# Running-ahead distances per stage, 24 whole fp32 columns in layer 1, and 32 gathers moved ahead, in a two-layer diffusion block with a product-key expert layer

## The chip, the cores and the metric

The kernel runs on one NeuronCore of one Trainium2 chip. The metric is the device time of one execution in microseconds; lower is better. The profile is one execution with a hardware trace. Engines are called as the profile calls them: PE is TensorE, DVE is VectorE, ACT is ScalarE, POOL is GpSimd, SP is SyncE.

## What is computed

Two layers of a block act on 256 latent tokens `x` and 256 context tokens `ctx`, each 1024 wide, all in fp32. Each layer has modulation from a condition vector, a mixer with three branches (differential attention, window attention with grouped heads, gated DeltaNet in chunks of 64), a gated merge, and an expert layer. The second layer updates the latent only; of the context it needs keys, values and the DeltaNet state.

```
for l in range(DEPTH):
    need_ctx = l < DEPTH - 1
    ...
    m, mc = token_mixer(h, hc, ...)
    x = x + gt1 * m
    x = x + gt2 * peer_ffn(modulate(x, norm2_g[l], sh2, sc2), peer_wq[l], peer_keys[l],
                           peer_u[l], peer_v[l])
    if need_ctx:
        xc = xc + gt1c * mc
        xc = xc + gt2c * peer_ffn(...)
return x
```

The expert layer `peer_ffn` picks, for each token and each of 8 heads, 16 of 16384 experts (top 16 of 128 first keys and of 128 second keys, then top 16 of the pairs), and returns the sum over experts e of softmax weight times gelu(h . u[e]) times v[e].

## The kernel before

The program is written as plain code against a recorder, `Rec`, which stands for the five engines. It notes each operation with its operands; `order()` is a list scheduler that then sets the order in which the operations of each engine are issued, and `emit()` issues them all from one line, L627. So every row of the trace has that line, and tiles tell the operations apart. `ps` is PSUM, `b` is a working tile in SBUF, `rows` a tile of 128 gathered table rows.

The scheduler goes by estimated costs and a priority: the place in the program, plus `base` (RBASE = -8000 makes routing urgent). An operation ahead of the oldest unfinished one of its lane is put off if it needs a tile and is further ahead than a distance (`FAR`, 80 units of estimated work), or if, beyond `NEAR` (20), it would leave fewer tiles than SPARE of its tag. Tags are b4 (36 tiles of 4 KB a partition), b2, b1 and ps (8 PSUM banks); `rows` and `ga` borrow slots of b4.

The stages in `run`: modulation of layer 0; the context through layer 0 (norm, projections by `w_in`, branches, merge, output projection); `peer_front`, the context's routing; `mix(0,0)`, the latent through layer 0; the latent's expert layer `peer_dense(0,0)`; layer 1 (`add_peer`, norm, keys, values and state of the context, then `mix(1,0)` and `peer_dense(1,0)` of the latent).

The context's experts (`peer_gather`) are lane -1, run beside the latent's work. For a block of 128 tokens, U gathers 128 times 128 rows of the first table (512 KB each, indirect DMAs that POOL issues); DVE multiplies each with h and sums. V then forms the weights `cf`, transposes them, gathers 128 times from the second table, PE multiplies with a selector `Z` (`ps<-rows,ga`), and ACT copies the result to a tile that SP stores in DRAM (`xd<-ga`). The order is U(0), V(0), U(1), V(1). `add_peer` of layer 1 loads what V stored.

The latent's experts are computed densely: for each of 128 columns (first keys), dU computes gelu of all 256 tokens against 128 rows of u, G (the weight of each token and expert, made in the stage "build" from one-hot rows by small matmuls and written to DRAM as `gd`) multiplies it on DVE, and dV multiplies with 128 rows of v. `pre` columns of dU (32 in layer 0, PRE1 = 64 in layer 1) stand ahead of the first dV.

A load in fp32 is mostly split: ACT casts it to the high half in fp32r, DVE subtracts to get the low half, and PE does three fp32r matmuls (`mm3`) for each product. A column in `u4` is left whole instead: one fp32 matmul against the unsplit transposed norm `hT[k][2]`, which the trace shows as two records. Before, `U4 = range(32)` makes the first 32 columns of layer 0 whole and layer 1 has none. In `first` of `peer_dense`:

```
if c0 in u4:
    for k in range(KT):
        nc.tensor.matmul(sp[:, i], u[:, k], hT[k][2], start=(k == 0), stop=(k == KT - 1))
    continue
uh, ul = self.split(u, ...)
self.mm3(sp[:, i], lambda k: (uh[:, k], ul[:, k]), lambda k: hT[k])
```

Of the kernel before, what the change touches and what calls it, by code (L numbers as in the profile page):

```python
# [41 lines left out]
WN = 32  # L42
U4, V4 = range(32), ()
WPOOL = ()
UP0, UP1 = (), ()
PRE1 = 64
# [7 lines left out]
GBASE, RBASE = 0, -8000  # L54
TAIL, FREE1 = 0, True
FREE = {"b4": 4, "b2": 2, "b1": 1, "ps": 0}
PRE = 32
LOAD = {"tensor": 1.0, "vector": 0.3, "scalar": 0.2}
NEAR, FAR, URGENT = 20.0, 80.0, 0.0

# [210 lines left out]
class Op:  # L271
    __slots__ = ("i", "eng", "meth", "args", "kw", "dur", "dma", "preds", "succ", "tiles", "prio",
                 "npred", "ready", "lab", "lane", "cw", "port", "free")

# [12 lines left out]
class Rec:  # L287
# [5 lines left out]
    def __init__(self, nc, pools, bufs):  # L293
        self.nc, self.pools, self.bufs = nc, pools, bufs
        self.ops, self.tiles = [], []
        self.tensor, self.vector = Eng(self, "tensor"), Eng(self, "vector")
        self.scalar, self.gpsimd, self.sync = Eng(self, "scalar"), Eng(self, "gpsimd"), Eng(self, "sync")
        self.base = 0
        self.lane, self.cw, self.free = 0, {}, False
        self.lab = ""  # L300
        self.why, self.prevt, self.inslot, self.fin = {}, {}, {}, {}
# [47 lines left out]
    def add(self, eng, meth, args, kw):  # L349
        o = Op()  # L350
# [36 lines left out]
        o.preds = list(preds)  # L387
        o.lane, o.free = self.lane, self.free
        o.cw = self.cw[o.lane] = self.cw.get(o.lane, 0.0) + o.dur * LOAD.get(eng, 0.0) * (URGENT if self.base == RBASE else 1.0)
# [14 lines left out]
    def order(self):  # L404
# [89 lines left out]
        def blocked(o):  # L494
            for t in o.tiles:
# [7 lines left out]
                if f > front:  # L503
                    keep = 0
                    if o.lane >= 0:
                        head = ops[lanes[o.lane][lpos[o.lane]]]
                        dist = o.cw - head.cw
                        free = o.free and lpos[-1] >= len(lanes[-1]) - TAIL
                        if dist > FAR and not free:
                            return "far"  # L510
                        if free and dist > NEAR:
                            keep = FREE.get(t.tag, 0)
                        elif dist > NEAR or o.lane != main:
                            keep = SPARE.get(t.tag, 0) + (LOADS if o.dma and t.tag == "b4" else 0)
                    if load[t.tag][front:f].max() + 1 > cap[t.tag] - keep:
                        return t.tag
# [114 lines left out]
class Kern:  # L631
# [1058 lines left out]
    def peer_gather(self, l, s, F):  # L1690

        nc = self.nc
        out = self.dram_x()
        for b in range(NB):
            self.lab(f"{l}{s} U{b}")
            dots = self.t("pdot", [P, P], bufs=1)
            h2 = self.t("ga", [P, D], bufs=3)
            nc.sync.dma_start(h2, F["hd"][b * P:(b + 1) * P, :])
            for j in range(P):
                r, _ = self.gather(self.I["u_tab"], F["eid"][j // 32][:, b].rearrange("p h k -> p (h k)")[:, j % 32:j % 32 + 1])  # L1700
                nc.vector.scalar_tensor_tensor(r, r, 1.0, h2, op0=OP.mult, op1=OP.mult, accum_out=dots[:, j:j + 1])
            self.lab(f"{l}{s} V{b}")
            cf = self.t("pcf", [P, P], bufs=2)
            nc.scalar.activation(cf, dots, AF.Gelu)
            nc.vector.tensor_tensor(cf, cf, F["gw"][:, b].rearrange("p h k -> p (h k)"), op=OP.mult)
            pt = self.ps([P, P], tag="psg")
            nc.tensor.transpose(pt, cf, self.id)
            cT = self.t("pcfT", [P, 4, 32], bufs=1)
            nc.scalar.copy(cT, pt.rearrange("p (q j) -> p q j", q=4))


            po = [self.ps([P, 512], tag="psg") for _ in range(2)]
            for j0 in range(0, 32, 8):
                Z = self.t("ga", [P, 8, 4, 32], bufs=3)
# [11 lines left out]
            acc = self.t("ga", [P, D], bufs=3)  # L1726
            for hf in range(2):
                nc.scalar.copy(acc[:, hf * 512:(hf + 1) * 512], po[hf])
            nc.sync.dma_start(out[b * P:(b + 1) * P, :], acc)
        return out  # L1730

# [39 lines left out]

    def run(self):
        self.setup()
        self.silu_c()
# [15 lines left out]
        if ADA1 == 4:  # L1790
            self.fill = fill
        self.whole = True
        _, (x, xs) = self.mix(0, 0, self.I["x"], pr, kv, S)
        self.whole = False
        self.dump("x0", x)
        self.layer_rows(1, pr1)
        self.nc.lane, self.nc.base = -1, GBASE
        acc = self.peer_gather(0, 1, F)
# [9 lines left out]
        self.lab("1 norm1")  # L1808
        self.nc.free = FREE1
# [4 lines left out]
        self.nc.free = False  # L1814
        _, (x, xs) = self.mix(1, 0, x, pr1, kv, S)
        self.dump("x2", x)
        self.peer_dense(1, 0, x, xs, pr1, self.out, pre=PRE1, up=UP1)

# [24 lines left out]
```

## Time and profile before

| what | value |
|---|---|
| time of the kernel, median of 3 runs | 3811.16 us (3800.89 to 3819.09) |
| the profiled execution, its own time | 3817.58 us |
| its span in the trace | 3815.8 us |
| mean granted clock of PE | 0.938 of full speed |
| PE busy | 3463.5 us (91%), 23800 instructions |
| weight loads of PE (PEld) busy | 2960.3 us (78%) |
| DVE busy | 2374.0 us (62%) |
| ACT busy | 1707.0 us (45%) |
| POOL busy | 818.8 us (21%) |
| DMA | 837.67 MB, mean 220 GB/s |

Busy shares are means over stages with different limits. So the span is cut into windows, with the busy time of each engine, the granted clock (a share of the full 2.4 GHz; 0.50 is 1.2 GHz) and the DMA share in each. The timeline lists an engine's instructions in order of time, merged when alike; brackets hold the idle time ahead of them and what ended it. "<-DVE b" means that the engine waited for DVE to write a tile `b`.

### The profile page before, as it was taken

Reading aid. Unit: us, or ns where it says so; the run is one execution under the profiler, and the core shown is the slowest. Engines: PE = TensorE matmul, PEld = TensorE weight load, DVE = VectorE, ACT = ScalarE, POOL = GpSimd, SP = SyncE. Lnnn points to the kernel's source line nnn. Section 1 sums busy time; section 2 is a strip of 40 time slices with the busy share of each in tenths; the row PEclk is TensorE's granted clock in tenths of the full one; section 3 lists DMA queues with packets and bytes.
Section 4 is the critical chain, followed back from the end, with each engine's and each line's share of the span. In section 5 each row is a group of like instructions: output and inputs, shape, how many; then the busy total and the mean of one; then the engine's idle time right before and its main releaser. Section 6 shows DMA issues by size and latency. Waiting matters only on the chain.

```text
span 3815.8 us, 62556 instructions
## 1 busy us (share of the span) xinstructions
PE 3463.5 (91%) x23800; PEld 2960.3 (78%) x23800; DVE 2374.0 (62%) x5288; ACT 1707.0 (45%) x3554; POOL 818.8 (21%) x716
## 2 busy tenths in 40 slices
PE   8999994987998987999999999998995789999999
PEld 6875993876797674788777778887795679889998
DVE  4542569887556783988544455645568963665554
ACT  4743441541543181343333347763543564444443
POOL 1010001476123434655444311101010000000000
PEclk9996997988899998999999998989997899999999
DMA  6346753597277889999899961212262364776562
GB/s 256 117 138 223 239 191 127 181 332 274 75 254 276 292 291 394 409 372 365 337 359 338 342 250 40 84 45 94 62 233 72 119 185 150 243 280 227 199 211 105
DMA packets 300956, 837.67 MB, mean 220 GB/s; under 512 B 26736, under 2 KB 96752, under 8 KB 300656
## 3 DMA queue, kind: packets, MB, share of 16 engines
q1 hardware_dynamic: 153168, 522.80, 38.6%
q0 software_dynamic: 73728, 268.47, 18.9%
q10 hardware_dynamic: 73760, 42.40, 3.7%
q8 instruction: 188, 3.08, 0.3%
q14 instruction: 112, 0.92, 0.1%
HBM read 792.67 MB, written 40.89 MB: 218 GB/s over the span
## 4 chain that ended last, share of the span: by engine, by line
PE 49%; DVE 4%; ACT 3%; issue 1%; DMA 1%; ACTq 0%; POOL 0%; POOLq 0%; DVEq 0%
PE ps L627 49%; ACT b L627 3%; DVE b L627 3%; DVE psi L627 0%; DVE psv L627 0%; ACTq L627 0%; DMA gd<-b 0%; DMA b<-in_v_tab 0%; DMA b<-in_u_cols 0%; DVE pii L627 0%; DVE pS L627 0%; DVE pci L627 0%; DVE dst L627 0%; DVE ga L627 0%; POOL qrs L627 0%
## 5 line engine op out<-in xcount | busy, mean ns | idle before, releaser
L627 PE MATMUL ps<-b,b 128*128 128x256 f32 (+4 forms) x18016 | 2761.0, 314 | 194.5 <-DVE b L627 121.6
L627 PEld LDWEIGHTS ps<-b,b 128*128 128x128 f32 (+1 forms) x18016 | 2452.5, 192 | 489.8 <-DVE b L627 141.9
L627 DVE TENSOR_TENSOR b<-b,b 128x1024 fp32r<-128x1024 f32 (+3 forms) x1218 | 1137.0, 977 | 718.5 <-ACT b L627 509.1
L627 ACT CAST b<-b 128x1024 fp32r<-128x1024 f32 (+1 forms) x918 | 850.2, 972 | 481.3 <-PE ps L627 341.0
L627 ACT COPY b<-ps 128x256 f32<-128x256 f32 (+3 forms) x896 | 289.2, 350 | 492.6 <-PE ps L627 483.5
L627 POOL DMA_INDIRECT rows<-in_u_tab,eid x256 | 349.4, 1365 | 321.5 <-DVE rows L627 232.7
L627 ACT ACTIVATE b<-ps 128x512 f32<-128x512 f32 (+1 forms) x266 | 137.5, 520 | 619.5 <-PE ps L627 609.6
L627 POOL DMA_INDIRECT rows<-in_v_tab,eidT x256 | 290.6, 1135 | 502.4 <-PE ps L627 442.4
L627 DVE SCALAR_TENSOR_TENSOR rows<-rows,ga 128x1024 f32<-128x1024 f32 x256 | 306.1, 1224 | 58.2 <-DMA rows<-in_u_tab,eid 58.2
L627 PE MATMUL ps<-consts,b 128*128 128x128 f32 (+1 forms) x1290 | 251.5, 312 | 84.1 <-DVE b L627 64.9
L627 PE MATMUL ps<-b 128*128 128x128 f32 (+1 forms) x2048 | 272.9, 301 | 37.8 <-ACT b L627 36.7
L627 PEld LDWEIGHTS ps<-b 128*128 128x128 f32 (+1 forms) x2048 | 231.6, 203 | 81.8 <-ACT b L627 60.0
L627 PEld LDWEIGHTS ps<-consts,b 128*128 128x128 f32 x1290 | 181.6, 179 | 131.9 <-issue 50.2
L627 DVE COPY_PREDICATED b<-masks,ps 128x64 f32<-128x64 uint8 (+1 forms) x416 | 83.2, 252 | 132.4 <-PE ps L627 129.4
L627 PE MATMUL ps<-rows,ga 128*32 128x512 f32 x1024 | 139.2, 599 | 7.2 <-DMA rows<-in_v_tab,eidT 7.2
L627 ACT COPY b<-b 128x128 f32<-128x128 f32 x384 | 108.0, 305 | 44.7 <-DVE b L627 42.3
L627 POOL TENSOR_TENSOR b<-b,b 128x512 f32<-128x512 f32 x24 | 45.5, 1896 | 351.7 <-DVE b L627 326.2
L627 DVE TENSOR_SCALAR b<-consts,b 128x128 f32<-128x128 f32 x384 | 110.3, 346 | 0.0
L627 DVE TENSOR_TENSOR b<-ps,b 128x128 f32<-128x128 f32 (+4 forms) x144 | 61.9, 455 | 72.3 <-PE ps L627 48.6
L627 DVE TENSOR_TENSOR b<-consts,b 128x512 f32<-128x512 f32 x128 | 87.0, 685 | 13.5 <-DMA gd<-b 8.6
L627 PE MATMUL ps<-b,cs 128*32 128x256 f32 x768 | 76.5, 460 | 11.6 <-DVE cs L627 11.6
L627 PEld LDWEIGHTS ps<-rows,ga 128*32 128x32 f32 x1024 | 29.2, 109 | 73.3 <-issue 45.0
(176 smaller groups left out, 1567.5 us busy)
## 6 DMA issues: line engine op xcount, KB each, us to landing
b<-in_u_cols SPq DMA_DIRECT2D x256, 512.0 KB, 5.5
b<-in_v_tab SPq DMA_DIRECT2D x256, 512.0 KB, 6.5
b<-in_w_in SPq DMA_DIRECT2D x184, 512.0 KB, 6.5
gd<-b ACTq DMA_DIRECT2D x64, 512.0 KB, 5.2
b<-gd SPq DMA_DIRECT2D x64, 512.0 KB, 5.7
b<-in_w_ada SPq DMA_DIRECT2D x48, 512.0 KB, 8.2
b<-in_w_ada SPq DMA_DIRECT2D x96, 256.0 KB, 4.6
b<-in_wq SPq DMA_DIRECT2D x48, 512.0 KB, 6.1
```

Of the source, the lines that this page charges most:

```text
L627: r = getattr(getattr(nc, o.eng), o.meth)(*[_real(x) for x in o.args], **{k: _real(x) for k, x in o.kw.items()})
```

## The change

First, the one distance FAR = 80 becomes a distance per stage, kept with each operation (`far`): 250 for modulation, context layer 0 and its routing; 150 for `mix(0,0)`; 200 for `peer_gather` and `peer_dense(0,0)`; 80 for layer 1's context; 150 for `mix(1,0)`; 200 for `peer_dense(1,0)`. A rule that let layer 1's context run ahead without limit once all gathers were done (`free`) is removed. Second, the first 24 columns of dU in layer 1 are whole. Third, `peer_gather` runs U(0), 32 gathers of U(1), V(0), the other 96 of U(1), V(1), with two tiles of sums in place of one, and V's weights get the urgent priority.

```diff
-U4, V4 = range(32), ()
+U4, U41, V4 = range(32), range(24), ()
...
-TAIL, FREE1 = 0, True
-FREE = {"b4": 4, "b2": 2, "b1": 1, "ps": 0}
+AHEAD = 32
...
-NEAR, FAR, URGENT = 20.0, 80.0, 0.0
+NEAR, URGENT = 20.0, 0.0
+
+FARS = (250, 150, 200, 80, 150, 200)
...
-                        free = o.free and lpos[-1] >= len(lanes[-1]) - TAIL
-                        if dist > FAR and not free:
+                        if dist > o.far:
                             return "far"
-                        if free and dist > NEAR:
-                            keep = FREE.get(t.tag, 0)
-                        elif dist > NEAR or o.lane != main:
+                        if dist > NEAR or o.lane != main:
                             keep = SPARE.get(t.tag, 0) + (LOADS if o.dma and t.tag == "b4" else 0)
...
-            dots = self.t("pdot", [P, P], bufs=1)
+                dots[b] = self.t("pdot", [P, P], bufs=2)
...
+        def V(b):
             self.lab(f"{l}{s} V{b}")
+            nc.base = RBASE
             cf = self.t("pcf", [P, P], bufs=2)
-            nc.scalar.activation(cf, dots, AF.Gelu)
+            nc.scalar.activation(cf, dots[b], AF.Gelu)
...
+        U(0, 0, P)
+        U(1, 0, AHEAD)
+        V(0)
+        U(1, AHEAD, P)
+        V(1)
...
-        self.peer_dense(1, 0, x, xs, pr1, self.out, pre=PRE1, up=UP1)
+        self.nc.far = FARS[5]
+        self.peer_dense(1, 0, x, xs, pr1, self.out, u4=U41, pre=PRE1, up=UP1)
```

The order on PE in layer 1's routing, before. `ps_5624` takes the next part of the query projection from the column of `wq` whose high half is `b4_5619` and whose low half is `b4_5620`; `ps_5817` to `ps_5840` are the first columns of dU.

```order
L627 MATMUL ps_5624_28565<-b4_5437_27974,b4_5619_28102 128x256
L627 MATMUL ps_5608_28569<-b1_5448_27145,b2_5607_28556 128x128 x4
L627 MATMUL ps_5817_28579<-b4_5436_27953,b4_5819_28168 128x256
L627 MATMUL ps_5817_28579<-b4_5437_27974,b4_5819_28168 128x256
L627 MATMUL ps_5825_28583<-b4_5436_27953,b4_5827_28212 128x256
L627 MATMUL ps_5825_28583<-b4_5437_27974,b4_5827_28212 128x256
L627 MATMUL ps_5832_28590<-b4_5436_27953,b4_5834_28259 128x256
L627 MATMUL ps_5832_28590<-b4_5437_27974,b4_5834_28259 128x256
L627 MATMUL ps_5840_28594<-b4_5436_27953,b4_5842_28305 128x256
L627 MATMUL ps_5840_28594<-b4_5437_27974,b4_5842_28305 128x256
L627 MATMUL ps_5624_28565<-b4_5436_27953,b4_5620_28845 128x256
```

The same place now; the query part is `ps_5622`, its low half `b4_5618`. The rows are the last ones ahead of the first matmul with that low half, and some of the first.

```order
L625 MATMUL ps_5622_28564<-b4_5439_27962,b4_5617_28145 128x256
L625 MATMUL ps_5606_28568<-b1_5446_26129,b2_5605_28555 128x128 x4
L625 MATMUL ps_5815_27951<-b4_5431_27964,b4_5816_27824 128x256 x4
L625 MATMUL ps_5815_27951<-b4_5430_27937,b4_5817_27911 128x256 x4
L625 MATMUL ps_5815_27951<-b4_5431_27964,b4_5817_27911 128x256 x4
L625 MATMUL ps_5819_28627<-b4_5430_27937,b4_5820_27966 128x256 x4
```

```order
L625 MATMUL ps_5836_28906<-b4_5431_27964,b4_5838_28464 128x256 x4
L625 MATMUL ps_5840_28954<-b4_5430_27937,b4_5841_28469 128x256 x4
L625 MATMUL ps_5840_28954<-b4_5431_27964,b4_5841_28469 128x256 x4
L625 MATMUL ps_5840_28954<-b4_5430_27937,b4_5842_28527 128x256 x4
L625 MATMUL ps_5840_28954<-b4_5431_27964,b4_5842_28527 128x256 x4
L625 MATMUL ps_5622_28564<-b4_5438_27953,b4_5618_28986 128x256
```

Whole columns (a row x4 is four fp32 matmuls of 256 tokens) have come ahead of the matmul with the low half: 15.5 of them by this point, all 24 by the first matmul of the build. Before, the 412 matmuls of the route and 176 of dU (7.3 columns of 24) stood ahead of the build.

The order on SP at the end of layer 0's build, before. `xd<-ga` is the store of V of block 0, `gd` is G on its way back, `in_v_tab` are rows of v.

```order
L627 DMA b4_3192_14195<-in_u_cols 128x1024
L627 DMA xd_2229_14300<-ga_2497_14289 128x1024
L627 DMA b4_3193_14302<-in_u_cols 128x1024
L627 DMA b4_3195_14304<-in_u_cols 128x1024
...
L627 DMA b4_3206_14347<-in_u_cols 128x1024
L627 DMA b4_3207_14358<-in_u_cols 128x1024
L627 DMA b4_3208_14378<-gd_2988_13185 128x1024
L627 DMA b4_3209_14380<-gd_2990_13713 128x1024
L627 DMA b4_3212_14383<-in_v_tab 128x1024
```

And now:

```order
L625 DMA b4_3206_14369<-in_u_cols 128x1024
L625 DMA b4_3207_14378<-in_u_cols 128x1024
L625 DMA b4_3208_14406<-gd_2988_13286 128x1024
L625 DMA b4_3212_14408<-in_v_tab 128x1024
...
L625 DMA b4_3258_14641<-in_v_tab 128x1024
L625 DMA b4_3261_14649<-in_v_tab 128x1024
L625 DMA xd_2229_14654<-ga_2531_14635 128x1024
L625 DMA b4_3266_14668<-in_v_tab 128x1024
```

The store now stands behind the last load of u, four loads of G and twelve of v, in place of ahead of nine loads of u.

The order on PE between the context's routing and the latent's norm in layer 0, before. `ps_1423` to `ps_1426` are the transposes of the latent's normed halves `b4_1411` and `b4_1412`; `ps_1382` is a part of the context's key scores; `ps_1405` transposes expert numbers for the gathers.

```order
L627 MATMUL ps_1423_6812<-consts_1_71,b4_1411_6089 128x128 x4
L627 MATMUL ps_1424_6819<-consts_1_71,b4_1411_6089 128x128 x4
L627 MATMUL ps_1382_6829<-b1_1201_5103,b2_1381_6815 128x128 x4
L627 MATMUL ps_1425_6837<-consts_1_71,b4_1412_6118 128x128 x4
L627 MATMUL ps_1426_6847<-consts_1_71,b4_1412_6118 128x128 x4
```

And now:

```order
L625 MATMUL ps_1423_6791<-consts_1_71,b4_1411_5675 128x128 x2
L625 MATMUL ps_1424_6796<-consts_1_71,b4_1411_5675 128x128 x2
L625 MATMUL ps_1425_6818<-consts_1_71,b4_1412_5688 128x128 x2
L625 MATMUL ps_1426_6825<-consts_1_71,b4_1412_5688 128x128 x2
...
L625 MATMUL ps_1405_6963<-consts_1_71,b1_1404_6959 128x128 x2
L625 MATMUL ps_1425_6818<-consts_1_71,b4_1412_5688 128x128 x2
L625 MATMUL ps_1426_6825<-consts_1_71,b4_1412_5688 128x128 x2
```

The transposes are now in two pieces each, and the last pieces of `b4_1412` stand behind the move of the expert numbers, which follows the last round of the search. On DVE all four scalings of the latent's norm stood ahead of the last search round; now three do.

## Rows read from the trace of the kernel before

**Rows 1.** The page's busy times, with their share of the span.

```profile
PE 3463.5 (91%) x23800; PEld 2960.3 (78%) x23800; DVE 2374.0 (62%) x5288; ACT 1707.0 (45%) x3554; POOL 818.8 (21%) x716
```

**Rows 2.** Windows, by stage; the first line names the columns.

```profile
core 0: us, PE busy (x) PEld busy (x) DVE busy (x) ACT busy (x) POOL busy (x), PEclk, DMA share, GB/s
...
650.00:1160.00 510.00, 459.91 (x3036) 394.69 (x3038) 376.92 (x819) 218.70 (x564) 219.72 (x191) 0.90 0.64 224
...
1432.00:1512.00 80.00, 56.92 (x226) 34.83 (x221) 18.71 (x31) 6.11 (x11) 37.18 (x37) 0.85 1.01 392
1512.00:1840.00 328.00, 305.02 (x1689) 260.76 (x1687) 292.49 (x430) 132.02 (x158) 172.34 (x113) 0.98 0.99 385
...
2862.00:3003.00 141.00, 81.94 (x651) 80.10 (x649) 119.07 (x528) 44.22 (x72) 0.90 (x2) 0.79 0.23 79
3003.00:3104.00 101.00, 76.47 (x534) 69.12 (x534) 88.32 (x255) 80.64 (x249) 0.00 (x0) 0.94 0.56 158
3104.00:3806.00 702.00, 700.09 (x4414) 632.60 (x4415) 374.14 (x440) 312.07 (x369) 0.00 (x0) 1.00 0.59 203
```

**Rows 3.** Waits of PE: us in total, times, the longest.

```profile
PE ps L627 <- DVE b L627: 187.0, 53, 45.5
```

**Rows 4.** Windows of five short stretches, columns as in rows 2.

```profile
310.00:350.00 40.00, 38.44 (x127) 23.61 (x128) 10.91 (x35) 13.19 (x42) 1.23 (x2) 0.50 0.20 61
350.00:385.00 35.00, 34.17 (x347) 21.95 (x348) 6.89 (x31) 11.97 (x34) 0.00 (x0) 0.85 0.95 336
900.00:1000.00 100.00, 73.56 (x345) 58.80 (x346) 77.09 (x149) 36.80 (x74) 46.41 (x42) 0.71 0.50 169
1000.00:1130.00 130.00, 130.00 (x1025) 116.56 (x1025) 72.97 (x110) 61.44 (x105) 20.22 (x15) 1.00 0.48 170
3110.00:3250.00 140.00, 140.00 (x1175) 140.00 (x1175) 62.35 (x53) 60.39 (x73) 0.00 (x0) 0.99 0.50 159
```

**Rows 5.** Timeline of PE in layer 0's expert layer: start, us, engine, what.

```profile
1199.14 14.08 PE L627 MATMUL ps<-b,b 128*128 128x256 f32 x64
```

**Rows 6.** Layer 1's routing: timeline of PE, then one DVE group by form.

```profile
2869.59 3.46 PE L627 MATMUL ps<-consts,b 128*128 128x128 f32 x16 [7.09 <-DVE b L627]
...
2966.93 28.66 PE L627 MATMUL ps<-b,b 128*128 128x256 f32 x222 [45.55 <-DVE b L627]
...
L627 DVE TENSOR_TENSOR b<-b,b 128x1024 fp32r<-128x1024 f32 x18 | 21.0, 1217 | 6.4 <-PE ps L627 6.4
```

**Rows 7.** Timeline of SP's DMA queue at the end of layer 0's build.

```profile
1432.76 0.33 SPq L627 DMA_DIRECT2D b<-in_u_cols  x1
1467.84 0.33 SPq L627 DMA_DIRECT2D xd<-ga  x1
1468.27 36.70 SPq L627 DMA_DIRECT2D b<-in_u_cols  x9
```

**Rows 8.** Timeline of PE, then DVE, in the same stretch.

```profile
1477.34 20.56 PE L627 MATMUL ps<-b,b 128*128 128x256 f32 x80 [14.75 <-DMA b<-in_u_cols]
1502.16 20.36 PE L627 MATMUL ps<-b,b 128*128 128x256 f32 x80 [4.26 <-DMA b<-in_u_cols]
...
1511.79 5.14 DVE L627 TENSOR_TENSOR b<-b,b 128x256 f32<-128x256 f32 x11 [19.45 <-DMA b<-gd]
```

**Rows 9.** DVE groups by form, 1512 to 1840 us: busy, mean ns.

```profile
L627 DVE SCALAR_TENSOR_TENSOR rows<-rows,ga 128x1024 f32<-128x1024 f32 x113 | 134.9, 1219 | 0.0
```

**Rows 10.** Timeline of POOL among the gathers of block 0's V.

```profile
1060.41 1.70 POOL L627 DMA_INDIRECT rows<-in_v_tab,eidT  x1 [68.90 <-PE ps L627]
```

**Rows 11.** Timeline of PE ahead of layer 1's context norm.

```profile
2221.87 28.30 PE L627 MATMUL ps<-b,b 128*128 128x256 f32 x192
...
2266.98 3.64 PE L627 MATMUL ps<-consts,b 128*128 128x128 f32 x16 [6.98 <-issue]
```

**Rows 12.** Timeline of PE at the end of the context's routing.

```profile
608.84 6.19 PE L627 MATMUL ps<-b,b 128*128 128x256 f32 x34 [34.08 <-DVE b L627]
...
642.10 8.01 PE L627 MATMUL ps<-b,b 128*128 128x256 f32 x46 [17.91 <-DVE b L627]
```

More of the change, by code (lines that the diff above doesn't have):

```diff
@@ L272 @@
     __slots__ = ("i", "eng", "meth", "args", "kw", "dur", "dma", "preds", "succ", "tiles", "prio",
-                 "npred", "ready", "lab", "lane", "cw", "port", "free")
+                 "npred", "ready", "lab", "lane", "cw", "port", "far")
 NAMES = []
@@ L298, in __init__ @@
         self.base = 0
-        self.lane, self.cw, self.free = 0, {}, False
+        self.lane, self.cw, self.far = 0, {}, 0.0
         self.lab = ""
@@ L387, in add @@
         o.preds = list(preds)
-        o.lane, o.free = self.lane, self.free
+        o.lane, o.far = self.lane, self.far
         o.cw = self.cw[o.lane] = self.cw.get(o.lane, 0.0) + o.dur * LOAD.get(eng, 0.0) * (URGENT if self.base == RBASE else 1.0)
@@ L1693, in peer_gather, with U @@
         out = self.dram_x()
-        for b in range(NB):
+        dots, h2 = {}, {}
+        def U(b, j0, j1):
             self.lab(f"{l}{s} U{b}")
-            dots = self.t("pdot", [P, P], bufs=1)
-            h2 = self.t("ga", [P, D], bufs=3)
-            nc.sync.dma_start(h2, F["hd"][b * P:(b + 1) * P, :])
-            for j in range(P):
+            if j0 == 0:
+                dots[b] = self.t("pdot", [P, P], bufs=2)
+                h2[b] = self.t("ga", [P, D], bufs=BORROW["ga"][1])
+                nc.sync.dma_start(h2[b], F["hd"][b * P:(b + 1) * P, :])
+            for j in range(j0, j1):
                 r, _ = self.gather(self.I["u_tab"], F["eid"][j // 32][:, b].rearrange("p h k -> p (h k)")[:, j % 32:j % 32 + 1])
-                nc.vector.scalar_tensor_tensor(r, r, 1.0, h2, op0=OP.mult, op1=OP.mult, accum_out=dots[:, j:j + 1])
+                nc.vector.scalar_tensor_tensor(r, r, 1.0, h2[b], op0=OP.mult, op1=OP.mult, accum_out=dots[b][:, j:j + 1])
+        def V(b):
             self.lab(f"{l}{s} V{b}")
+            nc.base = RBASE
             cf = self.t("pcf", [P, P], bufs=2)
-            nc.scalar.activation(cf, dots, AF.Gelu)
+            nc.scalar.activation(cf, dots[b], AF.Gelu)
             nc.vector.tensor_tensor(cf, cf, F["gw"][:, b].rearrange("p h k -> p (h k)"), op=OP.mult)
@@ L1709, in peer_gather @@
             nc.scalar.copy(cT, pt.rearrange("p (q j) -> p q j", q=4))
+            nc.base = GBASE
             po = [self.ps([P, 512], tag="psg") for _ in range(2)]
             for j0 in range(0, 32, 8):
-                Z = self.t("ga", [P, 8, 4, 32], bufs=3)
+                Z = self.t("ga", [P, 8, 4, 32], bufs=BORROW["ga"][1])
                 for j in range(8):
@@ L1725, in peer_gather @@
                             nc.tie(o, ds)
-            acc = self.t("ga", [P, D], bufs=3)
+            acc = self.t("ga", [P, D], bufs=BORROW["ga"][1])
             for hf in range(2):
@@ L1772, in run @@
     def run(self):
+        self.nc.far = FARS[0]
         self.setup()
@@ L1791, in run @@
             self.fill = fill
+        self.nc.far = FARS[1]
         self.whole = True
@@ L1796, in run @@
         self.layer_rows(1, pr1)
+        self.nc.far = FARS[2]
         self.nc.lane, self.nc.base = -1, GBASE
@@ L1808, in run @@
         self.lab("1 norm1")
-        self.nc.free = FREE1
+        self.nc.far = FARS[3]
         xs = self.add_peer(1, xc, acc, pr)
@@ L1813, in run @@
         S, _ = self.main(1, 1, hT, pr1, kv, None, False)
-        self.nc.free = False
+        self.nc.far = FARS[4]
         _, (x, xs) = self.mix(1, 0, x, pr1, kv, S)
         self.dump("x2", x)
-        self.peer_dense(1, 0, x, xs, pr1, self.out, pre=PRE1, up=UP1)
+        self.nc.far = FARS[5]
+        self.peer_dense(1, 0, x, xs, pr1, self.out, u4=U41, pre=PRE1, up=UP1)
 def body(tc, I, out, dbg=None):
```

## The prediction

> **What bounds the kernel now.** Read the busy times first: TensorE (PE) 3463.5 us of a span of 3815.8 [rows 1]. So at most 352 us of waiting can be won back; anything more must come from work removed or from the granted clock. Then take the windows, one per stage of the program [rows 2]. The reader should form span minus PE busy in each: 50 us in 650:1160, 23 in 1432:1512, 23 in 1512:1840, 59 in 2862:3003, 24 in 3003:3104 and 2 in 3104:3806. The last long stage is PE work alone, at a granted clock of 1.00; only fewer matmuls help there. The stage before it, 2862:3003, is the emptiest, and the waits say on whom: 187 us on VectorE (DVE), 45.5 of it in one piece [rows 3].
>
> **The profiled execution** took 3817.58 us, 6.4 above the median of 3811.16. The sum below is made against the former, and the 6.4 comes off at the end. A change under 0.5% (19 us) can't be told from none here.
>
> **1. 24 whole columns in layer 1.** A split column costs PE 24 fp32r matmuls; 1175 of them fill 140 us in the last stage [rows 4], 0.119 each, 2.86 a column. A whole one takes 14.08/4 = 3.52 in layer 0, where the same 64 records are four columns [rows 5]. So on PE each costs 0.66 more, 24 cost 15.8, and DVE and ACT are spared a subtraction and a cast each.
> Where it pays is layer 1's routing. Before, PE has dnorm, 412 route matmuls and the equal of 7.3 split columns ahead of the build of G. It stops 45.55 us at 2966.93 because the next matmul's low half waits behind the top-16 search on DVE [rows 6]; DVE is busy 119 of 141 us there, 21.0 of it in 18 subtractions of 128x1024 [rows 6]. In the new order 15.5 whole columns stand ahead of that matmul and all 24 ahead of the build; they need only their load and the latent's transposed tile.
> PE work from 2860 to the build then is 49 (412 x 0.119) + 84.5 (24 x 3.52) + about 5 (transposes and index moves), 138.5, plus 15 for waits that stay (7.09 before the transposes, small ones at the end [rows 6]): the build starts at about 3014 in place of 3003, some 11 to 14 us later. The columns behind the build fall from 128 - 7.3 = 120.7 to 104: 16.7 x 2.86 = 48 saved. Net **-33**. Bounds: -45 if the small waits are covered too, -20 if the loads of the 24 columns (each 512 KB; 12.6 MB in the 141 us that now move 79 GB/s) come late or the build, ACT-heavy with 80.64 of 101 us, gives something back. The two more tiles of 4 KB a partition cost nothing by themselves: their cover is the pool of 36, and if it is short, loads come later, which the -20 holds.
>
> **2. The store and the gathers around the end of layer 0's build.** SP's queue before has V of block 0's store ahead of nine loads of u columns. The store is issued at 1467.84, 35 us after the load ahead of it, and only then do the nine go out [rows 7]. PE waits 14.75 and 4.26 us for them [rows 8], and DVE's first multiply by G is at 1511.79, after a wait on G's load that stands behind the nine [rows 8]. In the new order all 32 u loads, four of G and twelve of v rows stand ahead of that store. So up to 27 us of start (1512 back to about 1485) are to be had.
> The second part is DVE in 1512:1840, busy 292 of 328, of which 113 products for the gathers take 134.9, 1.22 each [rows 9]. In the new order 96 stand there: 17 x 1.22 = 21 us less. But PE's work is not less: idle is 23 + 23 us in these two windows, and that is the ceiling, 46. I take 19 (both waits on u) + 13 of the second 23, **-32**; bounds -46 and 0, the latter if the transfers pace the stretch: DMA share is 1.01 and 392 GB/s in 1432:1512 and 0.99 after it [rows 2].
>
> **3. The 32 gathers moved ahead.** They go where GpSimd stands still: 68.90 us before 1060.41, waiting for PE to free V rows [rows 10]. Their DVE products (32 x 1.22 = 39 us, and 9 more of block 0 ahead of layer 0's norm) go into 650:1160, where DVE is busy 377 of 510 us [rows 2]. Block 0's V gathers follow later, and V of block 1, whose result layer 1's norm needs, ends later against PE: its last batch stands some 15 us of PE work ahead of the norm's transposes, against 38 before (2221.87 to 2266.98 less the 6.98 idle, [rows 11]). From the last gathered matmul to the transposes the trace has 45 us with 38 filled; the bare chain (store, load, multiply, add) I estimate from it at 26 to 28. So 10 more are left open: **+5** with part filled by other columns; bounds -20 (chain not longer, fill kept) and +30 (the 27 us of preparation that now lie between the first chain's steps in layer 1 move behind them, and nothing covers).
>
> **4. The distances per stage.** Context layer 0, distance 250 for 80: loads of the rest of the modulation start earlier. In 310:350 DMA is at 0.20 and PE at a clock of 0.50, with 38.44 busy; 350:385 is then almost all modulation at 0.95 DMA [rows 4]. Before, 72 of 160 of its matmul rows stand behind the last window attention, in the new order at most 6. Half of 38.44 is 19 us, if the full clock (2.4 GHz) is back: **-10**; bounds -30 (35 us tail all covered) and +8.
> Layer 0's latent norm: before, PE waits 34.08 and 17.91 us for the context's search, then starts on the latent's projections at 642-656 [rows 12]. In the new order one of four scalings of the norm stands behind the last search round, and the second half of the transposes behind that: a round is about 23 us on DVE, with nine more gather products about 28. PE starts that much later, and takes some of the 50 us idle of 650:1160 back: **+15**; bounds -10 and +30.
>
> One more thing bears on part 3. The rows show 0.48 to 0.50 of DMA and 170 GB/s in 900:1130 [rows 4], so I price the moved transfers at nothing. The Trainium skill, "DMA: Bandwidth & Descriptors", section "Issuing engines are not separate DMA queues", says that transfers started by ScalarE, SyncE or GpSimd all run on the same 16 engines and interleave; by it the gathers delay the merge's weights, which is rival C.
>
> **Sum**: -33 - 32 + 5 - 10 + 15 = -55; 3817.6 - 55 = 3762.6, less 6.4: **3756 us**.
>
> **The rivals.**
> A. More is won: the tail and clock of part 4 in full (-30), the late start absorbed (0), all 46 of part 2, -40 of part 1, +8 of part 3: -108, **3703**. For it: idle of that size is there. Against: each part must reach its bound at once.
> B. Layer 0's end stays paced by transfers: part 2 gives 3 in place of 32, as the share near 1.0 says: -26, **3785**. Against: the 32 moved gathers (16.8 MB, 43 us at 392 GB/s) leave just that stretch.
> C. The 32 gathers queue with the merge's weights: the 43 us come in 900:1130, where PE already waits and runs at 0.71 in the first 100 us [rows 4]: -55 + 43 = -12, **3799**. Against: half of DMA is free there.
> D. Slower: DVE becomes the bound of 650:1160. 41 products x 1.22 = 50 us are put in front of attention's own DVE work, PE starts 28 later, and about 20 of PE work falls to the half clock: +100 in place of +15, against 75 won elsewhere (33 + 32 + 10): +25 to +30, **3838**. It decides from 75 on. For it: DVE is at 74% there and at 77 of 100 in 900:1000 [rows 4]. Against: 133 us of DVE are free in 650:1160.
> That the change doesn't do what it says is excluded: the new order has the 24 columns and the 32 gathers in place.
>
> **How the numbers follow.** Forecast 0.52, A 0.13, B 0.17, C 0.10, D 0.08. The forecast's own range is 3735 to 3780. The whole range goes from A to past C, 3703 to 3806, and leaves out D and half of A. Faster by over 19 us (under 3792): forecast, A, and 0.12 of B: 0.77. Within 0.5%: the rest of B and C: 0.15. Slower: D, 0.08.
>
> **What would show it.** Right: no PE wait over 20 us between 2860 and the build; about 104 columns behind it, so the last stage some 48 us shorter; no wait on u columns near 1470; DVE's first multiply by G near 1485 on the old scale; PE's latent projections starting 20 to 30 us later after the routing. Wrong: a new long wait of PE on DVE between 650 and 1160, PE waiting for w_in or branch weights near 1000, a gap over 20 us before layer 1's norm transposes, or 1432:1840 as long as now.

## The result and the profile after

The changed kernel takes 3763.47 us (median of 4 runs, 3751.17 to 3777.71) beside 3811.64 before: a ratio of 0.9867, 95% interval 0.983 to 0.9904. Measured a second time, beside other kernels, it was 0.9857 (0.982 to 0.9895). The prediction was 3756, a ratio of 0.9855.

The page's first part, of the changed kernel (busy us, share of the span, instructions; its span is 3759.3, its own time 3761.2):

```profile
PE 3461.5 (92%) x23608; PEld 2957.8 (79%) x23608; DVE 2344.6 (62%) x5264; ACT 1692.7 (45%) x3530; POOL 815.0 (22%) x716
```

PE's busy time is that of before to 2 us [rows 1]: the whole columns add some 13 us (experiment 2), and a higher granted clock (0.947 for 0.938) and other shifts take as much away. So of the 56 us that the span lost, all but 2 are idle time of PE. Windows of the changed kernel, cut where the same instructions stand (length, PE, PEld, DVE, ACT, POOL busy, granted clock, DMA share, GB/s):

```profile
503.40:721.50 218.10, 134.08 (x883) 122.88 (x883) 190.22 (x682) 58.29 (x112) 59.10 (x57) 0.80 0.42 141
721.50:1033.80 312.30, 287.52 (x1755) 233.40 (x1756) 260.44 (x579) 141.93 (x432) 192.09 (x156) 0.87 0.74 255
1419.30:1486.10 66.80, 45.17 (x210) 24.75 (x209) 3.74 (x9) 7.05 (x12) 25.06 (x27) 0.85 1.05 402
1486.10:2227.10 741.00, 718.90 (x4417) 588.41 (x4417) 469.77 (x641) 295.36 (x351) 296.23 (x228) 0.98 0.91 346
...
2844.22:2992.93 148.71, 140.13 (x857) 129.91 (x857) 109.71 (x520) 40.79 (x75) 0.90 (x2) 0.98 0.36 121
2992.90:3749.40 756.50, 728.65 (x4544) 651.52 (x4545) 442.19 (x678) 374.29 (x592) 0.00 (x0) 0.99 0.59 201
```

The fifth row, layer 1's routing, answers to 2862:3003 of before [rows 2]: PE is idle 9 us there in place of 59. The first is the opposite: between the context's output projection and the latent's preparation, PE is idle 84 us, where it was 59 before:

```profile
527.21:717.07 189.86, 131.13 (x882) 121.84 (x883) 164.89 (x644) 55.70 (x116) 35.23 (x39) 0.84 0.39 130
```

The stages between the same matmuls, in the profile before, in two profiles of the changed kernel, and by the prediction:

| from the last point to | before | changed | second | change | predicted |
|---|---|---|---|---|---|
| context's routing starts | 536.9 | 514.5 | 513.8 | -22 | -10 |
| latent's preparation in layer 0 ends | 180.2 | 207.0 | 208.5 | +27 | +15 with the next |
| latent's output projection ends | 441.5 | 421.2 | 436.4 | -20, -5 | |
| layer 0's build ends | 272.9 | 276.6 | 283.1 | +4, +10 | 0 |
| layer 0's dV ends | 828.5 | 807.7 | 809.1 | -21 | -32 |
| layer 1's context norm ends | 10.6 | 19.9 | 19.9 | +9 | +5 with the next |
| layer 1's output projection ends | 591.9 | 597.3 | 597.2 | +5 | |
| layer 1's build starts | 141.2 | 148.7 | 148.7 | +7 | -33 with the next |
| end | 812.1 | 766.4 | 766.4 | -46 | |

Two profiles of one kernel agree to 2 us in seven of nine rows, and differ by 15 and 7 in the third and fourth. In the third it is mostly PE's granted clock: 0.87 in 721:1034 of the first profile, 0.84 in the same stage of the second:

```profile
722.40:1047.40 325.00, 297.85 (x1755) 241.66 (x1754) 261.23 (x579) 142.61 (x431) 183.85 (x156) 0.84 0.71 246
```

Same 1755 matmuls, same idle time to 3 us, 10 us more of busy time. In the fourth row the busy time is the same to 2 us, and it is PE's idle time that goes from 19 to 27 us. So in stages like these a difference of some 10 us between two profiles may be none.

### The profile page after: what moved, and what is told of

It is laid out like the page before. It is cut to its first block, busy times and chain, and to the rows that moved or that the text cites. A ratio compares the mean times of both kernels' runs of the same rounds, so it can differ in the third digit from the quotient of the medians.

```text
span 3759.3 us, 62186 instructions
## 1 busy us (share of the span) xinstructions
PE 3461.5 (92%) x23608; PEld 2957.8 (79%) x23608; DVE 2344.6 (62%) x5264; ACT 1692.7 (45%) x3530; POOL 815.0 (22%) x716
## 4 chain that ended last, share of the span: by engine, by line
PE 79%; DVE 7%; ACT 5%; DMA 4%; issue 2%; ACTq 1%; POOL 1%; SPq 0%; POOLq 0%; DVEq 0%
PE ps L625 79%; ACT b L625 5%; DVE b L625 4%; DMA gd<-b 2%; DVE rows L625 1%; ACTq L625 1%; DMA b<-in_v_tab 1%; POOL rows L625 0%; DMA rows<-in_v_tab,eidT 0%; DVE psi L625 0%; DMA b<-in_w_ada 0%; DVE dst L625 0%; DVE psv L625 0%; DMA rows<-in_u_tab,eid 0%; DVE pii L625 0%
## 5 line engine op out<-in xcount | busy, mean ns | idle before, releaser
L625 PE MATMUL ps<-b,b 128*128 128x256 f32 (+5 forms) x17824 | 2764.0, 316 | 139.7 <-DVE b L625 72.1
L625 PEld LDWEIGHTS ps<-b,b 128*128 128x128 f32 (+2 forms) x17824 | 2452.1, 191 | 437.4 <-ACT b L625 99.7
L625 DVE TENSOR_TENSOR b<-b,b 128x1024 fp32r<-128x1024 f32 (+3 forms) x1194 | 1105.4, 968 | 757.7 <-ACT b L625 530.4
L625 ACT CAST b<-b 128x1024 fp32r<-128x1024 f32 (+1 forms) x894 | 827.0, 969 | 565.7 <-PE ps L625 353.7
L625 POOL TENSOR_SCALAR qrs<-qrs 128x8 f32<-128x8 f32 (+1 forms) x24 | 12.4, 517 | 337.1 <-DVE qrs L625 302.3
```

The lines of the kernel that those rows point to most:

```text
L625: r = getattr(getattr(nc, o.eng), o.meth)(*[_real(x) for x in o.args], **{k: _real(x) for k, x in o.kw.items()})
```

## The experiments

Ratios are to the kernel before, run on the same chip, with 95% intervals; 0.001 is 3.8 us.

**1. The whole columns alone.**

```diff
-U4, V4 = range(32), ()
+U4, U41, V4 = range(32), range(24), ()
...
-        self.peer_dense(1, 0, x, xs, pr1, self.out, pre=PRE1, up=UP1)
+        self.peer_dense(1, 0, x, xs, pr1, self.out, u4=U41, pre=PRE1, up=UP1)
```

> The kernel before with the 24 whole columns of layer 1 alone; in its order on PE 23 whole columns stand ahead of layer 1's build in place of the equal of 7.3 split ones, and nothing differs up to layer 1's routing. Theory (the wait for the top-16 search is filled): 33 to 39 us less than before, about 3775, no wait of over 20 us on PE in layer 1's routing, the build starting 8 to 14 us later after the norm's transposes, and 45 to 48 us less from the build's start to the end. Rival (the columns' loads come late, or the build gives part back): at most 20 us less.

Measured: 0.9907 (0.9878 to 0.9935), about 36 us less, as the theory said. Its profile, of the slowest of ten runs, shows less: the build starts 7 us later, and from there to the end it is 31 us shorter, not 45 to 48.

**2. The reverse**, the changed kernel without them:

```diff
-U4, U41, V4 = range(32), range(24), ()
+U4, U41, V4 = range(32), (), ()
```

> The changed kernel without its 24 whole columns: in its order all up to layer 1's routing is as in the changed kernel, and the routing is as before. Theory (the parts add up): 33 to 39 us over the changed kernel, about 3800, with PE's wait of about 45 us in layer 1's routing back. Rival (the gain in layer 1 comes from the distance of 200 there, not from the columns): within 10 us of the changed kernel.

Measured: 0.995 (0.9916 to 0.9983), 32 to 36 us over the changed kernel by its two ratios. PE's timeline in layer 1's routing, first in the changed kernel, with the columns:

```profile
2851.71 3.59 PE L625 MATMUL ps<-consts,b 128*128 128x128 f32 x16 [7.49 <-DVE b L625]
2855.13 128.90 PE L625 MATMUL ps<-b,b 128*128 128x256 f32 x800
...
2984.08 7.07 PE L625 MATMUL ps<-b,b 128*128 128x256 f32 x32
...
2992.93 2.26 PE L625 MATMUL ps<-b 128*128 128x128 f32 x16 [1.10 <-ACT b L625]
```

and in the changed kernel without them:

```profile
2871.43 3.68 PE L625 MATMUL ps<-consts,b 128*128 128x128 f32 x16 [8.62 <-DVE b L625]
2875.19 49.70 PE L625 MATMUL ps<-b,b 128*128 128x256 f32 x414
2968.97 26.37 PE L625 MATMUL ps<-b,b 128*128 128x256 f32 x210 [44.08 <-DVE b L625]
...
3003.45 6.75 PE L625 MATMUL ps<-b 128*128 128x128 f32 x33 [1.27 <-ACT b L625]
```

800 matmuls without a gap against 414, a wait of 44.08 for the search, and 210. The build starts 141 us after the transposes in the one, 132 in the other, and the rest is 47 us shorter. From layer 1's output projection to the end PE is busy 868.8 us with the columns and 855.7 without: 13 us more, or 0.55 a column, and idle 52 us less. The columns pay by themselves, with or without the other parts. The distance of 200 isn't needed for it, but with it they pay more in the last stage: that is 802 us before, 803 here, 771 with the columns alone (experiment 1) and 756 in the changed kernel.

**3. The moved gathers alone** (`peer_gather` of the changed kernel, all else of before).

```diff
+AHEAD = 32
...
+        U(0, 0, P)
+        U(1, 0, AHEAD)
+        V(0)
+        U(1, AHEAD, P)
+        V(1)
```

> The kernel before with the moved gathers alone (32 of block 1's first table ahead of block 0's second table, two tiles of sums, urgent weights); all 32 loads of u columns stand ahead of block 0's store, as in the changed kernel. Theory: PE's two waits on u columns near 1470 (19 us) go and 13 more of the stretch to 1840; layer 0's expert layer ends 20 to 32 us earlier, and layer 1's norm gives back up to 10: 15 to 30 us less than before, about 3790. Rival B (transfers pace the end of layer 0's build): within 8 us of before. Rival C (the early gathers delay the merge's weights): PE waits on weights between 900 and 1130, up to 43 us, and a time of 3810 to 3830.

Measured: 0.989 (0.9834 to 0.9946), 42 us less with a wide interval (21 to 64); more than the theory's range at the median. Neither B nor C: PE's waits on merge weights stayed away. This run has the two tiles of sums and the urgent weights too, so the order of the gathers is not told apart from them.

**4. The distances alone**, all six of the change, with the rule for layer 1's context removed as there.

```diff
+FARS = (250, 150, 200, 80, 150, 200)
...
-                        free = o.free and lpos[-1] >= len(lanes[-1]) - TAIL
-                        if dist > FAR and not free:
+                        if dist > o.far:
```

> The kernel before with the six distances in place of the one, and the rule for layer 1's context removed, and nothing else. Theory: the context's first stages end 20 us earlier, the latent's projections of layer 0 start 28 us later against that, of which some 20 come back until the merge; layer 0's expert layer still has the store ahead of eight loads of u; in layer 1 the context's chains lose their filling work (about 15 us). Sum about -5: 3800 to 3815. Rival: the running ahead is what makes the gain, 25 us or more less than before. Rival D (DVE becomes the bound of the stretch from 650 to 1160): 10 us or more over before.

Measured: 1.003 (1.0009 to 1.0051), 11 us more. Running ahead, as these six numbers set it, costs. That is the number of rival D but not its way: in the latent's stage after the routing PE is idle 32 us, 48 before. The stage of the late norm takes 219 us for 190. What the removed rule does by itself no run tells.

**5. The store taken off SP's queue**, in the kernel before. PE's order stays.

```diff
-            nc.sync.dma_start(out[b * P:(b + 1) * P, :], acc)
+            nc.scalar.dma_start(out[b * P:(b + 1) * P, :], acc)
```

> The kernel before with one thing changed: the two stores of the gathered sums are issued by ACT in place of SP. PE's order is that of before. Theory (the store held up SP's queue and the nine loads of u behind it): the waits of 14.75 and 4.26 us on u columns go, DVE's first multiply by G comes 15 to 27 us earlier, and the time is 10 to 25 us less. Rival B (the transfers themselves pace this stretch, or the loads wait for tiles): the loads go out earlier or not, but DVE's first multiply moves by less than 8 us, and the time is within 8 us of before.

Measured: 0.9994 (0.9971 to 1.0017). Rival B holds. SP's queue, then PE, then DVE at the end of layer 0's build, in this kernel:

```profile
1434.46 54.01 SPq L627 DMA_DIRECT2D b<-in_u_cols  x11
1511.33 3.79 SPq L627 DMA_DIRECT2D b<-gd  x2
...
1477.55 31.35 PE L627 MATMUL ps<-b,b 128*128 128x256 f32 x144
1522.73 0.80 PE L627 MATMUL ps<-b,b 128*128 128x512 f32 x1 [13.83 <-ACT b L627]
...
1516.56 1.43 DVE L627 TENSOR_TENSOR b<-b,b 128x256 f32<-128x256 f32 x4 [13.35 <-DMA b<-gd]
```

The u loads go out at 1434, 33 us earlier than the nine of before [rows 7], and PE's waits of 14.75 and 4.26 are gone [rows 8]. But eleven loads take 54 us to issue, DVE's first multiply stands at 1516.56 (1511.79 before, and all of this profile runs 5 us later by then), and PE waits 13.83 in front of dV in their place. The window that the loads share with the gathers of U(1) is full:

```profile
1434.50:1516.60 82.10, 66.34 (x302) 41.15 (x294) 18.55 (x31) 9.56 (x22) 40.87 (x39) 0.93 1.04 406
```

DMA share 1.04 at 406 GB/s: here transfers set the pace, and the place of the store in the queue sets nothing.

**6. Whole columns and gathers, without the distances**: the edits of experiments 1 and 3 together.

```diff
+U4, U41, V4 = range(32), range(24), ()
+AHEAD = 32
```

> The kernel before with the 24 whole columns and the moved gathers, but the one distance of 80 and the rule for layer 1's context as before. Theory (the two parts add, and the distances as a whole cost 11 us): 0.9907 x 0.989 = 0.980 of before, 25 us or so under the changed kernel. Rival (the gathers need the distances to pay): 0.987 or more.

Measured: 0.9836 (0.9807 to 0.9864). Better than the changed kernel's 0.9867 and 0.9857 at the median, by 8 to 12 us, not by the 25 expected; the two parts alone would multiply to 0.980. Against experiment 5, whose order up to layer 1's routing is that of before, on the same chip, three stages differ: the latent's expert norm to layer 0's build end, 258.9 to 243.5; dV's end 824.7 to 827.1; layer 1's context norm to its preparation, 204.5 to 193.2. The first two hold the same work, shifted: block 0's V matmuls have left the routing and lie behind the build. So what is won at that end is 13 us, not 32. The windows, first of experiment 5, then of this kernel:

```profile
1181.80:1440.70 258.90, 244.00 (x1673) 189.80 (x1676) 204.54 (x786) 118.84 (x308) 93.60 (x90) 0.99 0.80 276
1440.70:2265.40 824.70, 772.94 (x4641) 620.01 (x4638) 512.84 (x719) 300.23 (x366) 367.36 (x275) 0.98 0.94 363
2276.00:2480.50 204.50, 198.04 (x1610) 178.28 (x1611) 124.61 (x312) 145.81 (x433) 26.95 (x35) 0.92 0.18 58
```

```profile
1184.60:1428.10 243.50, 229.96 (x1607) 185.57 (x1605) 202.32 (x784) 116.40 (x302) 74.88 (x74) 0.99 0.77 259
1428.10:2255.20 827.10, 788.80 (x4692) 621.36 (x4692) 471.51 (x645) 298.75 (x359) 327.15 (x265) 0.98 0.93 352
2273.20:2466.40 193.20, 190.08 (x1611) 171.88 (x1611) 124.16 (x312) 145.68 (x433) 22.86 (x35) 0.98 0.19 62
```

In the first two rows together PE is busy the same time to 2 us and idle 15 us less, and by GB/s times length 16.6 MB fewer are moved: the 32 gathers. The third row is another thing. The matmuls are the same and the idle time is 6 and 3 us; 8 of its 11 us are busy time at another clock, 0.92 and 0.98. In experiment 1, whose order there is that of before, the same stage has 0.86:

```profile
2286.69:2502.01 215.32, 208.59 (x1610) 186.43 (x1611) 124.97 (x312) 146.75 (x433) 26.94 (x35) 0.86 0.18 55
```

So one order alone gives this stage 204 to 215 us, and whether its 11 us belong to the gathers isn't shown.

**7. With the first distance** (250 up to layer 0's context output projection, 80 from the routing on).

```diff
+        self.nc.far = 250
         self.setup()
...
+        self.nc.far = 80
         F = self.peer_front(0, 1, xs, pr)
```

> As the kernel with whole columns and moved gathers, and the distance of 250 for the first stages alone (setup to the context's output projection in layer 0); from the context's routing on the distance is 80 again, and in the order the latent's norm stands ahead of the last search round as before. Theory (the first distance wins 20 us of clock, the later ones lose it in the routing): 15 to 20 us under the kernel with whole columns and gathers alone; about 0.975 of before. Rival (what the context wins is lost in the routing anyway, since DVE's search sets its end): within 8 us of that kernel.

Measured: 0.983 (0.9803 to 0.9856), 2 us under experiment 6: the rival's number, but not by the rival's way. In the profiles the routing starts 23 us earlier (516.6 for 540.0) and the lead is still 26 us at layer 1's norm; 16 of it are gone at the end. 12 of them go between layer 1's context norm and its routing, by the clock: with the same matmuls to one PE is busy 14 us longer there, at 0.93 for 0.98 and 0.95. The lead itself is partly clock. Its first stage takes 372 us at 0.96; experiments 10 to 12, with the same 2782 matmuls in it, take 383 to 385 at 0.91 and 0.92, beside 387 in experiment 6. Whether the distance brings the clock on either side or chance does stays open.

**8. The latent's norm made urgent** in the changed kernel.

```diff
+        self.nc.base = -4000 if l == 0 else 0
         hT = self.norm1(xt, pr, s)
+        self.nc.base = 0
```

> The changed kernel with the latent's norm in layer 0 at a higher priority, so that in the order it stands ahead of the context's last search round again, as before; the rest is placed anew by the scheduler. Theory (the late norm costs 28 us, of which some 5 to 8 come back until the merge): PE's idle time in the routing falls from 84 to about 59 us, and the time is 15 to 25 us under the changed kernel. Rival (DVE's queue is what matters, and the search only ends later): the same idle time, and a time within 8 us.

Measured: 0.9916 (0.9885 to 0.9946), some 19 to 23 us over the changed kernel. PE's idle time from the context's output projection to the latent's preparation fell to 59.7 us as expected, but the scheduler placed everything behind anew, and the stages behind are longer: the merge 121 us for 109 and 111 in the two profiles of the changed kernel, layer 0's build 286 for 277 and 283, layer 1's context 225 for 208, there with the same 1627 matmuls at a clock of 0.88 for 0.92. So this run tells nothing on the norm's price; experiment 11 tells more.

**9. The changed kernel again**, as a base for the next three.

> The changed kernel once more, beside the three below, as their base. 0.987 of before, inside the interval of its first measurement.

Measured: 0.9857 (0.982 to 0.9895).

**10. Two distances**: experiment 7 with 200 in layer 1's expert layer.

```diff
+        self.nc.far = 200
         self.peer_dense(1, 0, x, xs, pr1, self.out, u4=U41, pre=PRE1, up=UP1)
```

> Whole columns and moved gathers, the distance of 250 up to the context's output projection in layer 0, 200 in layer 1's expert layer, 80 in all between, and the rule for layer 1's context kept. Theory (these two distances are the ones that pay: the first brings clock, the last some 14 us after the start of layer 1's build, and the middle ones cost the late norm and the lost filling work): 10 to 18 us under the kernel with the first distance alone, 0.979 to 0.981 of before, 20 to 30 us under the changed kernel. Rival (the differences between the profiles after the build are the clock's chance): 0.983 of before.

Measured: 0.9811 (0.9783 to 0.9839), 3757.52 us (3753.02 to 3762.28) beside 3783.03 for the changed kernel. The lowest of all medians, about 18 us under the changed kernel by the ratios; their intervals still touch. The last stage is 757 us, as in the changed kernel (756), where experiments 6 and 7, whose order has 23 whole columns ahead of the build in place of 24, have 770 and 773: this distance seems to pay. By the runs it is 7 us under experiment 7, and their intervals overlap. Like those two, this kernel keeps the rule for layer 1's context.

**11. The latent's distance added**, on experiment 10.

```diff
+        self.nc.far = 150
         _, (x, xs) = self.mix(0, 0, self.I["x"], pr, kv, S)
...
+        self.nc.far = 80
         acc = self.peer_gather(0, 1, F)
```

> As the kernel with two distances, with 150 in place of 80 for the latent's layer 0 up to its output projection; in the order a part of the latent's norm stands behind the context's last search round, as in the changed kernel. Theory (this distance is what makes the late norm, and it costs more than it brings): PE's idle time in the routing rises from 58 to 84 us, and the time is 10 to 25 us over the kernel with two distances. Rival (the late start comes back until the merge, as the changed kernel's profile seemed to show): within 8 us.

Measured: 0.9893 (0.986 to 0.9927), 31 us over experiment 10. Windows from the context's output projection to the latent's preparation, to its last attention, and from the merge's end to the build's end, without and with it:

```profile
517.80:706.30 188.50, 130.23 (x882) 120.77 (x880) 164.84 (x644) 55.62 (x116) 36.23 (x39) 0.84 0.39 131
706.30:1047.80 341.50, 293.79 (x1765) 238.95 (x1765) 283.44 (x615) 138.35 (x423) 206.45 (x178) 0.84 0.75 264
...
1153.13:1419.04 265.91, 239.21 (x1649) 191.47 (x1650) 208.26 (x793) 121.47 (x313) 82.05 (x84) 0.96 0.78 266
```

```profile
519.50:737.10 217.60, 133.71 (x882) 123.07 (x881) 189.01 (x681) 57.48 (x111) 57.42 (x57) 0.80 0.45 150
737.10:1061.90 324.80, 297.12 (x1756) 241.22 (x1756) 261.02 (x579) 142.56 (x433) 184.03 (x156) 0.84 0.71 245
...
1168.86:1457.56 288.70, 256.02 (x1704) 194.81 (x1706) 208.98 (x793) 123.18 (x312) 98.67 (x100) 0.95 0.79 272
```

Idle time 84 for 58, the stage 29 us longer; 17 of it come back in the next, so the late norm costs 12 us net there. The profiles part again behind the merge: the stage to the build's end is 23 us longer. 56 more matmuls of gathered rows stand in it (386 for 330), and PE is busy 17 us longer. Later stages give some back, and the profiles end 19 us apart, the runs 31. Late norm and this distance go together; 31 us is the price of the distance, and the late norm is a part of it.

**12. 64 gathers in place of 32**, on experiment 10.

```diff
-AHEAD = 32
+AHEAD = 64
```

> As the kernel with two distances, with 64 gathers of block 1's first table ahead of block 0's second in place of 32. Theory (transfers pace the end of layer 0's build, and gathers moved ahead of it relieve it): another 16.8 MB leave that stretch, and V of block 1 ends earlier against layer 1's norm; 5 to 20 us under the kernel with 32. Rival (DVE becomes the bound between 650 and 1160, or the relief is used up): the same time within 5 us, or more.

Measured: 0.9915 (0.9885 to 0.9944), 40 us over experiment 10, against the theory. The window of the merge and output projection (the one of experiment 10 ahead, then this kernel's), and DVE's costliest forms in it:

```profile
1047.80:1153.10 105.30, 102.56 (x861) 99.30 (x861) 72.62 (x93) 49.94 (x68) 29.71 (x19) 1.00 0.76 269
```

```profile
1047.50:1185.90 138.40, 115.85 (x860) 107.74 (x862) 111.97 (x158) 49.01 (x68) 74.94 (x51) 0.93 0.87 324
```

```profile
L628 DVE TENSOR_TENSOR b<-b,b 128x1024 fp32r<-128x1024 f32 x39 | 52.2, 1362 | 8.0 <-issue 4.0 <-PE ps L628 2.4 <-ACT b L628 1.5
L628 DVE SCALAR_TENSOR_TENSOR rows<-rows,ga 128x1024 f32<-128x1024 f32 x39 | 48.3, 1268 | 0.0
```

39 products of gathered rows (48.3 us) stand between the 39 subtractions that PE's merge matmuls wait for. DVE goes from 73 of 105 us to 112 of 138, PE's idle time from 3 to 23, and PE's clock falls from 1.00 to 0.93. That is rival D's mechanism, not at 32 gathers but at 64, and in the merge rather than in attention. The relief that the theory spoke of came too: PE's wait ahead of layer 1's context norm, 10.73 us in experiment 10, is gone, and that stage takes 1.3 us for 18.

## Why the prediction was right, point by point

The time, 7 us from the forecast, and the sign are right. Part 1 held by its own reason; parts 2 and 3 and the distances as a whole did not come as priced, and that their misses cancelled is luck.

**Part 1 held.** -33 was said; alone the columns gave 36, taken away 32 to 36. The steps are in the table: the build 7 us later (11 to 14 said), then 46 less (48 said). But some 15 of the 46 came with the distance of 200, for which the sum had no term: with the old one the last stage is 29 to 32 us shorter (experiments 1, 6 and 7). A column cost PE 0.55 us more, not 0.66 (experiment 2). The build started sooner than said because of the 15 us of waits that I left standing 8.6 are left. Before, the idle 45.55 us were also a stretch at a clock of 0.53; with the columns the whole routing ran at 0.98.

**Part 2 failed in its step.** "SP's queue before has V of block 0's store ahead of nine loads of u columns" is so in the order, but it isn't what set the time: experiment 5 took the store away and won nothing. The "27 us of start" were not to be had from the store's place, as the bound at 0 of that term and rival B had it. In the changed kernel the wait on u is gone and another stands in its place. SP's queue, DVE, PE and ACT there:

```profile
1410.39 38.48 SPq L625 DMA_DIRECT2D b<-in_u_cols  x7
...
1457.94 1.43 DVE L625 TENSOR_TENSOR b<-b,b 128x256 f32<-128x256 f32 x4 [43.43 <-DMA b<-gd]
...
1486.05 10.30 PE L625 MATMUL ps<-b,b 128*128 128x512 f32 x36 [16.86 <-ACT b L625]
...
1482.71 1.04 ACT L625 CAST b<-b 128x1024 fp32r<-128x1024 f32 x1 [14.74 <-DMA gd<-b]
```

DVE's first multiply did come 54 us earlier, 42 of it counted from the build's end, but PE waits 16.86 where it had waited 19: for a cast on ACT, which stood behind the stores of G (`gd<-b`). The stage from the build's end to dV's end got 21 us shorter, by less idle time (43.7 us for 53.1) and less work in it. Some of that work went into the stage ahead, which took 4 and 10 us more in the two profiles. So of -32 the two stages together show 17 and 9.

**Part 3 was undervalued with part 2.** Together they were -27; the gathers alone measured 42 less, 21 to 64. That the moved gathers "leave just that stretch", said there against rival B, is seen: 16.6 MB and 13 us less in experiment 6. The rest of the 42 is in no stage that one profile tells from the clock's spread, and stays open. The wait before layer 1's norm has the size that I said, 10 us more, but not from the gathers alone. It is 9.24 more in the changed kernel (16.22 for the 6.98 of [rows 11]):

```profile
2243.29 3.64 PE L625 MATMUL ps<-consts,b 128*128 128x128 f32 x16 [16.22 <-issue]
```

With the gathers alone (experiment 3) it is 3.75 more, and with the distances alone (experiment 4), without the moved gathers, 10.11 more: 10.73 and 17.09, the length less PE's busy time in the windows of this stage, in this order:

```profile
2253.72:2271.66 17.94, 7.21 (x49) 6.66 (x47) 12.80 (x22) 7.00 (x15) 1.27 (x3) 0.71 0.77 303
```

```profile
2261.92:2282.66 20.74, 3.65 (x17) 3.28 (x16) 17.69 (x24) 6.42 (x15) 4.25 (x5) 0.62 0.58 188
```

So that this term came out is luck as well.

**Part 4 was undervalued as a cost.** +5 was said; alone the distances cost 11 (3 to 20). Of its two terms, the clock at the start came back more fully than said in the profile (-22; clock 0.96 in 0:364), but in the runs experiment 7 finds only 2 us of it. The late norm was seen in the order and its start is right ("PE starts that much later": 27 us). "takes some of the 50 us idle of 650:1160 back" is right as well: 20 and 5 us come back in the two profiles of the changed kernel and 17 in experiment 11, which leaves some 7, 23 and 12 where 15 was said. What the sum had no term for is what the middle distances do behind the merge: by experiment 11 the latent's distance costs 31 us in all. The rows of the late norm are those of the changed kernel, where the third wait is for the late step:

```profile
562.58 22.19 PE L625 MATMUL ps<-b,b 128*128 128x256 f32 x164 [24.15 <-DVE b L625]
...
619.80 13.47 PE L625 MATMUL ps<-b,b 128*128 128x256 f32 x100 [30.99 <-DVE b L625]
...
657.65 1.76 PE L625 MATMUL ps<-consts,b 128*128 128x128 f32 x6 [17.93 <-DVE b L625]
```

**The rivals.** A didn't come: no part reached its bound. B is right as a mechanism and wrong as a time, since the gathers that leave the stretch relieve it by 13 us. C didn't show: DMA share is 0.74 in 721:1034 of the changed kernel, and PE waits for no weights there or in the merge, so the price of nothing held. In experiment 5 the stores went from SP's queue to ACT's and loads went out 33 us earlier, and all of it shared 406 GB/s at a share of 1.04, with no time won. The Trainium skill, "DMA: Bandwidth & Descriptors", section "Issuing engines are not separate DMA queues", says that transfers started by ScalarE, SyncE or GpSimd run on the same 16 DMA engines and interleave; that run agrees. D's mechanism is seen with 64 gathers and not with 32.

The parts alone would give 36 + 42 - 11 = 67 us less; together they give 48 to 55. The lowest time is that of the change without its middle distances and with the rule for layer 1's context (experiment 10); of the middle distances only the latent's was set by itself.

## What to carry to other kernels

Fill the longest wait of the bounding engine with work that needs only what is already there, even if that work costs it more: 0.55 us a column more bought 36 us. Before you price a queue's order, look at the DMA share of the window: here, at 1.0, the order only moved the wait; 16.6 MB taken out of the stretch shortened it, by 13 us; and with 64 gathers DVE, which has to work on them, had no room in the place they went to. A table of numbers set at once is to be taken apart: here the kernel with two of six distances had the lowest time, and one of the others cost 31 us.

## What the runs showed of the hardware

Runs of one kernel differ, and the slower ones have the lower granted clock of PE. The changed kernel's first four runs go 3751.17 us at a mean clock of 0.950, 3761.2 and 3765.74 at 0.947, 3777.71 at 0.941; the kernel before, beside experiment 5, from 3805.71 at 0.942 to 3833.42 at 0.936. The spread is some 27 us in both, half of this change. The clock is low behind idle time, as in the kernel before, where PE had 47.69 of 48 us busy at 1.00 and then, with next to nothing to do, 0.53:

```profile
2873.00:2921.00 48.00, 47.69 (x402) 47.24 (x402) 39.46 (x193) 24.16 (x35) 0.00 (x0) 1.00 0.33 108
2921.00:2967.00 46.00, 0.45 (x5) 0.25 (x3) 45.18 (x241) 0.06 (x1) 0.00 (x0) 0.53 0.00 0
```

It was at 0.50 also with PE busy 38.44 of 40 us by the records [rows 4], with few and long matmuls (127) in it. So a stage made shorter early doesn't keep its gain for sure (experiment 7), and a difference of 10 us between two profiles in a stage whose clock differs says little (the third row of experiment 6).
